# Weight forms split two at a time, and two up tiles of every three taken in seven products (a hybrid retention, gating and conv-MLP layer)

## The chip, the cores and the metric

The kernel runs on one core of a Trainium2 chip. The metric is the device time of one execution in microseconds, taken as the median of three runs. Beside it there is one execution recorded by the hardware profiler; its rows are what the working below is made of.

The engines are named as the profile names them: PE is the matrix engine (TensorE; PEld its weight loads), DVE the vector engine (VectorE), ACT the scalar engine (ScalarE), POOL is GpSimd, and SP the engine that issues most of the transfers. "Instruction on line 85" is written L85.

## What is computed

The layer takes x of 512 tokens by 1024 features in float32 and has two halves:

```python
def reference(x, ...):
    h = _rmsnorm(x, g_pre_mix)
    proj = h @ w_in
    q, k, v, g, u, sv, a_ret, a_sgu = jnp.split(proj, ...)
    y_ret = _retention_branch(q, k, v, g, ret_decay_logit, w_ret_o)
    y_sgu = _sgu_branch(u, sv, sgu_ln_g, sgu_ln_b, w_spatial, b_spatial, w_sgu_o)
    merged = jax.nn.sigmoid(a_ret) * y_ret + jax.nn.sigmoid(a_sgu) * y_sgu
    x = x + _rmsnorm(merged @ w_out, g_post_mix)
    h2 = _rmsnorm(x, g_pre_ffn)
    x = x + _rmsnorm(_conv_gated_mlp(h2, w_up, conv_w, conv_b, w_down), g_post_ffn)
    return x

def _conv_gated_mlp(h, w_up, conv_w, conv_b, w_down):
    hid = h @ w_up                          # 1024 -> 5632
    hid = ... three-tap convolution over the tokens, per feature ... + conv_b
    a, b = jnp.split(hid, 2, axis=-1)
    return (jax.nn.gelu(a) * b) @ w_down    # 2816 -> 1024
```

The change concerns above all the up product `h @ w_up` of the second half.

## The kernel before

**Three matmuls per product.** Every matrix is float32. The matrix engine reads it as two parts in its faster format: `hi`, a copy in that format, and `lo`, what is left (`split`, L83 to L85: the copy on ScalarE at L78, the subtraction on VectorE at L85). A product then takes hi·hi, hi·lo and lo·hi. All weights are loaded as float32 tiles of 128 x 1024 (512 KB) and split on the way.

**The weight stream.** The list `units` (L92 to L116) says in which order weights are used. `w_get` (L198) hands out the next unit and prepares those ahead of it: it goes on until about eight to ten slots' worth of units (`LOOK` = 4) is prepared. A unit of size 2 takes two slots (hi and lo of 1024 columns), a single form of size 1 takes one. Raw weights go through four buffers (`raw_tile`, L119), the split ones through nine slots (`slot`, tag w4, L122). Three kinds of unit matter here. `blk` is one weight tile of 128 output features, whole. `q` and `t` are the two units of a pair in the down product: `q` has the weights as they come (768 columns to split), `t` four sums of them (1024 columns). The third kind are the forms of a pair.

**A pair and a block.** An output tile of 128 features by 512 tokens can be made as a *block* (`f_block`, L635): 8 steps over the 1024 input features, three matmuls of 512 columns each, 24 in all. Two such tiles can be made together as a *pair* (`Pair`, L646 to L705): the product of 1024 x 256 weights with 1024 x 512 activations is cut two by two and made in seven half-size products in place of eight (the Strassen-Winograd scheme), each of four steps with three matmuls of 256 columns: 84 matmuls of 256 columns in place of 48 of 512. The seven weight matrices are the *forms* B11, B21, T1, T2, T3, T4, B22, four of them sums of the others. `w_form` (L152 to L170) makes each when it comes up: B11 loads two raw tiles; T1 computes T1 and T3 on VectorE (L163, L164) and starts T2 on GpSimd (L165); T4 is a GpSimd add as well (L167). Every form is split by itself, 512 columns at a time, into one slot. `part1` makes four products and the first half of the results (the add at L679), `part2` one product (the subtraction at L690), `part3` the last two products (the subtraction at L702). The activations' forms S1 to S4 are made once, by `h2_forms`. The `u` stage and the two gate stages ahead use the same class, four pairs in each, with the gate stages laying two blocks into each pair.

**The up stage.** There are 22 gated tiles (NF), each of two 128-feature output tiles, one of the `a` half and one of the `b` half. Tiles 0 to 3 and 20 and 21 are two blocks each. Tiles 4 to 19 are taken in *couples* (COUPLES, L38): tile i is a pair, tile i + 1 two blocks, and the blocks lie between the pair's parts, so that the forms have time to be made:

```python
            p.part1()
            o = [f_block(h2h, h2l, KD)]
            p.part2()
            o.append(f_block(h2h, h2l, KD, p.part3))   # part3 in the middle of this block
            tile_done(i, p.t)
            tile_done(i + 1, o)
```

`tile_done` (L972) takes a tile through the convolution (`conv`, L928: one scaling on ScalarE, then two steps over 511 columns on VectorE, L933 and L937, for each of its two halves) and the gate (`gated`, L943: the activation on ScalarE, a product on VectorE at L946). At some tiles (7, 11, 13, 17, and from 19 on) it also makes the activation forms of one pair of gated tiles for the down product (`down_forms`, L953: some ten operations on VectorE, L959 to L962 and splits).

**The down product.** 22 tiles are taken as nine pairs (`products`, one `q` and one `t` unit each, seven products of two token tiles with three matmuls each, 42 of 256 columns a pair, L1033) and four whole tiles, twice, for the two halves of the output features.

**What sets the order.** The program is written as one stream; the framework orders each engine's instructions by its own schedule and adds the waits. On each engine instructions run in that order. Buffers are reused round robin: the matrix engine's results lie in eight banks, `tmp` tiles (pair results, convolution results) in six buffers. The transfers of the weights are issued by SP in the stream's order, each as soon as a raw buffer is free.

Of the kernel before, what the change touches and what calls it, by code (L numbers as in the profile page):

```python
# [13 lines left out]
ALU = mybir.AluOpType  # L14

P = 128
# [18 lines left out]
WHOLE = NF - 2 * DP  # L35
EAGER = 7
UP0 = DOWN0 - 2 * NF
COUPLES = [(i, i + 1) for i in range(4, 20, 2)]  # L38

PRE, FFNG, LNG, LNB = 0, 8, 16, 24  # L40
CW, CB = 32, 32 + 3 * 2 * NF
# [5 lines left out]
def tile_block(ctx: ExitStack, tc, xT, x, wall, par, cs, wsp, bsp, gpost, gffn, out):  # L47
# [14 lines left out]
    def tmp(n="tmp", shape=(P, S)):  # L62
        return sb.tile(list(shape), F32, tag="tmp", bufs=6, name=nm(n))
# [19 lines left out]
    def split(hi, lo, src):  # L83
        copy(hi, src)
        nc.vector.tensor_sub(lo, src, as32(hi))  # L85
# [2 lines left out]

    RES1 = NW - 22 - 44
    RES0 = RES1 - RES_OUT  # L90
    FORMS = ("B11", "B21", "T1", "T2", "T3", "T4", "B22")
    units = []  # L92
    i = 0
    while i < NW:
        pair = [(f, i) for f in FORMS]
        if U0 <= i < GATE0:
            units += pair
            i += 2
        elif GATE0 <= i < GATE1:
            units += pair[:4] + [("blk", i + 2)] + pair[4:] + [("blk", i + 3)]  # L100
            i += 4
        elif i == UP0 + 2 * COUPLES[0][0]:
            for a, b in COUPLES:
                pair = [(f, UP0 + 2 * a) for f in FORMS]
                units += pair[:4] + [("blk", UP0 + 2 * b)] + pair[4:] + [("blk", UP0 + 2 * b + 1)]
            i = UP0 + 2 * COUPLES[-1][1] + 2
        elif i == DOWN0:
            for _ in range(2):
                pairs = [[("q", i + j), ("t", i + j)] for j in range(DP)]
                whole = [[("blk", i + DP)], [("blk", i + DP + 1)]]  # L110
                for u in pairs[:4] + whole[:1] + pairs[4:6] + whole[1:] + pairs[6:] if i == DOWN0 else pairs + whole:
                    units += u
                i += DP + WHOLE // 2
        else:
            units.append(("blk", i))
            i += 1  # L116
    w_ready, w_pos, w_held, w_raw = {}, [0, 0], [0], {}

    def raw_tile():  # L119
        return sb.tile([P, 1024], F32, tag="raw", bufs=4, name=nm("raw"))  # L120

    def slot(n, at=0, w=1024):  # L122
        return sb.tile([P, 1088], F32R, tag="w4", bufs=9, name=nm(n))[:, at : at + w]
# [27 lines left out]

    def w_form(form, i):  # L152

        if form == "B11":
            a, b = raw_tile(), raw_tile()
            nc.sync.dma_start(a, wall[i])
            nc.sync.dma_start(b, wall[i + 1])
            w_raw["B11"], w_raw["B12"] = a[:, :S], a[:, S:]
            w_raw["B22"], w_raw["B21"] = b[:, :S], b[:, S:]
        elif form == "T1":  # L160
            t = raw_tile()
            w_raw["T1"], w_raw["T2"], w_raw["T3"], w_raw["T4"] = t[:, :S], t[:, S:], w_raw["B12"], t[:, S:]
            nc.vector.tensor_add(w_raw["T1"], w_raw["B11"], w_raw["B12"])  # L163
            nc.vector.tensor_add(w_raw["T3"], w_raw["B12"], w_raw["B22"])  # L164
            nc.gpsimd.tensor_tensor(out=w_raw["T2"], in0=w_raw["T1"], in1=w_raw["B22"], op=ALU.add)  # L165
        elif form == "T4":
            nc.gpsimd.tensor_tensor(out=w_raw["T4"], in0=w_raw["T2"], in1=w_raw["B21"], op=ALU.add)  # L167
        w = slot("wf", 16)
        split(w[:, :S], w[:, S:], w_raw[form])
        return w[:, :S], w[:, S:]  # L170

    def w_down(form, i):

# [19 lines left out]
        return w_block(u[1]) if u[0] == "blk" else (w_down if u[0] in "qt" else w_form)(*u)  # L193

    def w_size(u):
        return 2 if u[0] in ("blk", "q", "t") else 1

    def w_get(look=LOOK):  # L198

        i = w_pos[0]  # L200
        w_pos[0] += 1
        room = 2 * look + (2 if w_size(units[i]) == 2 else 0)
        n = sum(w_size(u) for u in units[i : w_pos[1]])
        while w_pos[1] < len(units) and (w_pos[1] <= i or n + w_size(units[w_pos[1]]) <= max(room, 9 if look == LOOK else 0)):
            u = units[w_pos[1]]
            w_ready[w_pos[1]] = w_unit(u)
            w_pos[1] += 1
            n += w_size(u)
        return w_ready.pop(i)
# [425 lines left out]
    def f_block(ah, al, n, between=None):  # L635

        wh, wl = w_get()
        o = ps()
        for k in range(n):
            if between and k == n // 2:  # L640
                between()
            c = slice(k * P, (k + 1) * P)
            mm3(o, wh[:, c], wl[:, c], ah[k], al[k], k == 0, k == n - 1)
        return o

    class Pair:  # L646
# [5 lines left out]
            self.h, self.l, self.forms = a or (xh, xl, forms)  # L652
            self.b = [ps() for _ in range(3)]

        def product(self, b, act, first, w=None):
            wh, wl = w or w_get()
            o = self.b[b][:, T0]
            for k in range(4):
                c = slice(k * P, (k + 1) * P)
                h_, l_ = act(k)  # L660
                for n, (w_, a_) in enumerate(((wh, h_), (wh, l_), (wl, h_))):
                    nc.tensor.matmul(  # L662
                        o, w_[:, c], a_, start=first and k == n == 0, stop=k == 3 and n == 2,
                        skip_group_check=True,
                    )
            return o
# [6 lines left out]

        def part1(self):
            c0, c1 = self.t
            o = self.product(0, self.x(0, T0), True)
            copy(c0[:, T0], o)
            o = self.product(1, self.x(4, T0), True)
            v.tensor_add(c0[:, T0], o, c0[:, T0])  # L679
            self.product(2, self.s("S1"), True)  # L680
            o = self.product(0, self.s("S2"), False)
            copy(c1[:, T0], o)
            if self.scale is not None:
                v.tensor_mul(c0[:, T0], c0[:, T0], self.scale[:, T0])

        def part2(self):
            c0, c1 = self.t
            o = self.product(0, self.s("S3"), False)
            copy(c1[:, T1], o)
            v.tensor_sub(c1[:, T1], self.b[2][:, T0], c1[:, T1])  # L690
            self.w = w_get(), w_get()

        def part3(self):
            c0, c1 = self.t
            o = self.product(0, self.x(4, T1), False, self.w[0])
            if self.scale is None:
                copy(c0[:, T1], o)
            else:
                v.tensor_mul(c0[:, T1], o, self.scale[:, T1])
                nc.scalar.activation(out=c0, in_=c0, func=self.func)  # L700
            o = self.product(2, self.s("S4"), False, self.w[1])
            v.tensor_sub(c1[:, T0], o, c1[:, T0])  # L702
            if self.scale is not None:
                v.tensor_mul(c1, c1, self.scale)
                nc.scalar.activation(out=c1, in_=c1, func=self.func)  # L705
# [265 lines left out]

    def tile_done(i, o):  # L972
        gated(*(conv(t, 2 * i + s_) for s_, t in enumerate(o)))
        if i < COUPLES[-1][1]:
            if i in (7, 11, 13, 17):
                down_forms(len(dforms))
        elif len(dforms) < EAGER:
            down_forms(len(dforms))
# [11 lines left out]
            split(h_, l_, s_)  # L990
            h2forms[n] += [(h_[:, t], l_[:, t]) for t in (T0, T1)]

    couples = dict(COUPLES)
    i = 0
    while i < NF:
        if i in couples:
            p = Pair(None, lambda: tmp("c"), (h2h, h2l, h2forms))
            p.part1()
            o = [f_block(h2h, h2l, KD)]
            p.part2()  # L1000
            o.append(f_block(h2h, h2l, KD, p.part3))
            tile_done(i, p.t)
            tile_done(i + 1, o)
            i += 2
        else:
            o = []
            for e in (2 * i, 2 * i + 1):
                o.append(early_o[e] if e < EARLY else f_block(h2h, h2l, KD))
            tile_done(i, o)
            for k in {0: (0,), 1: (2,)}.get(i, ()):  # L1010
                h2_forms(k)
            i += 1
# [150 lines left out]
def _parts(a, n, w):  # L1163

    k = a.shape[0] // P
    return a.reshape(k, P, n, w).transpose(2, 1, 0, 3).reshape(n, P, k * w)
# [11 lines left out]
def _inter(a, b):  # L1178
    return np.stack([a, b], 1).reshape(2 * a.shape[0], *a.shape[1:])


def _two(a):

    b = _parts(a, 8, P).reshape(4, 2, P, 2, S)
    return np.stack([
        np.concatenate([b[:, 0, :, 0], b[:, 1, :, 0]], -1), np.concatenate([b[:, 1, :, 1], b[:, 0, :, 1]], -1),
    ], 1)


def _up(a):  # L1190

    for i, _ in COUPLES:
        b, c = a[2 * i].reshape(P, 2, S), a[2 * i + 1].reshape(P, 2, S)
        a[2 * i : 2 * i + 2] = np.stack([
            np.concatenate([b[:, 0], c[:, 0]], -1), np.concatenate([c[:, 1], b[:, 1]], -1),
        ])
    return a


def _gates(a, w):  # L1200

    return np.concatenate([_two(a), _parts(w, 8, P).reshape(4, 2, P, 1024)], 1).reshape(16, P, 1024)


def _quads(a):
# [76 lines left out]
```

## Time and profile before

| | |
|---|---|
| median of three runs | 830.31 us (830.2 to 830.32) |
| the profiled execution | 831.73 us, its span 830.0 us |
| granted TensorE clock in it | 0.997 |
| start of tile 4 in the up stage | 523.42 us |
| start of the down product | 712.08 us |

The profile is read as follows. A row of a timeline is: start, duration (both us), engine, line, operation, the tile written and the tiles read, shape. On a pipelined engine durations of neighbours overlap, so the cost of an instruction in a dense stretch is the distance to the next start. A row of the chain is start, duration, engine, tile, line and count. A row of the waits is engine, tile and line that waited, on what, and then total, times and longest in us. A row of the windows is the stretch, its length, and for each engine its busy time with the count of instructions, then the granted clock, the DMA engines' share and GB/s.

### The profile page before, as it was taken

How to read it: one execution, taken by the hardware profiler on the slowest of the kernel's cores; microseconds unless marked ns; L12 is line 12 of the kernel's file. 1: busy time of each engine (PE TensorE's matmuls, PEld its weight loads, DVE VectorE, ACT ScalarE, POOL GpSimd, SP SyncE). 2: the span in 40 equal slices, each digit the busy share in tenths (PEclk: the TensorE clock that was granted, in tenths of full speed). 3: DMA queues.
4: the chain of work that ended last, by engine and by line, in shares of the span. 5: the costliest groups of instructions: out<-in, count | busy, mean ns of one | idle time of the engine just before them, and what ended most of it. 6: DMA issues, size and time to landing. Idle time of an engine off the chain costs nothing.

```text
span 830.0 us, 13260 instructions
## 1 busy us (share of the span) xinstructions
PE 819.0 (99%) x5152; PEld 738.5 (89%) x5152; DVE 657.9 (79%) x1100; ACT 439.6 (53%) x769; POOL 101.4 (12%) x102
## 2 busy tenths in 40 slices
PE   9999999999999999999999999999999999999995
PEld 7888888888899999999988898899999998999995
DVE  7479898877898777767765568979799889987967
ACT  6635445546665444444445685556566566554531
POOL 0010000102121111132211211210201200000001
PEclk9999999999999999999999999999999999999998
DMA  8733222213233332233359111233233341233344
GB/s 289 248 115 102 77 77 76 77 51 101 69 101 126 102 102 88 91 101 102 104 162 339 46 54 61 102 102 102 102 102 102 102 153 51 77 115 106 118 147 153
DMA packets 29215, 93.24 MB, mean 112 GB/s; under 512 B 3360, under 2 KB 4000, under 8 KB 29152
## 3 DMA queue, kind: packets, MB, share of 16 engines
q1 hardware_dynamic: 26928, 86.85, 31.5%
q0 software_dynamic: 1360, 4.46, 1.6%
q10 hardware_dynamic: 864, 1.09, 0.4%
q8 instruction: 40, 0.66, 0.3%
q14 instruction: 23, 0.19, 0.1%
HBM read 88.19 MB, written 4.19 MB: 111 GB/s over the span
## 4 chain that ended last, share of the span: by engine, by line
PE 91%; DVE 6%; issue 1%; ACT 1%; POOL 0%; DMA 0%; POOLq 0%; ACTq 0%; DVEq 0%
PE ps L662 24%; PE ps L212 12%; PE ps L213 12%; PE ps L214 12%; PE ps L1033 8%; PE ps L473 5%; PE ps L474 5%; PE ps L475 5%; PE ps L812 2%; PE ps L810 2%; PE ps L811 2%; PE ps L735 1%; DVE fl L85 1%; PE ps L274 1%; DVE dl L85 1%
## 5 line engine op out<-in xcount | busy, mean ns | idle before, releaser
L85 DVE TENSOR_TENSOR wl<-raw,wh 128x1024 fp32r<-128x1024 f32 (+1 forms) x93 | 108.0, 1171 | 52.7 <-PE ps L662 29.4
L78 ACT ACTIVATE wf<-raw 128x512 fp32r<-128x512 f32 x140 | 85.0, 627 | 98.0 <-PE ps L213 41.4
L85 DVE TENSOR_TENSOR wf<-raw,wf 128x512 fp32r<-128x512 f32 x140 | 108.7, 791 | 25.3 <-ACT wf L78 24.1
L662 PE MATMUL ps<-sh,wf 128*128 128x256 f32 x640 | 122.5, 281 | 0.0
L78 ACT ACTIVATE wh<-raw 128x1024 fp32r<-128x1024 f32 (+2 forms) x95 | 93.2, 990 | 38.5 <-DMA raw<-wall 18.5
L662 PEld LDWEIGHTS ps<-sh,wf 128*128 128x128 f32 x640 | 101.7, 188 | 0.8 <-ACT u L78 0.2
L212 PE MATMUL ps<-h2h,wh 128*128 128x512 f32 (+1 forms) x256 | 92.7, 365 | 0.3 <-ACT h2h L880 0.3
L213 PE MATMUL ps<-h2l,wh 128*128 128x512 f32 (+1 forms) x256 | 92.7, 364 | 0.0
L214 PE MATMUL ps<-h2h,wl 128*128 128x512 f32 (+1 forms) x256 | 92.5, 362 | 0.0
L662 PE MATMUL ps<-sl,wf 128*128 128x256 f32 x320 | 89.9, 281 | 0.0
L473 PE MATMUL ps<-wh,xh 128*128 128x512 f32 x192 | 75.0, 391 | 0.0
L474 PE MATMUL ps<-wl,xh 128*128 128x512 f32 x192 | 74.9, 390 | 0.0
L475 PE MATMUL ps<-wh,xl 128*128 128x512 f32 x192 | 74.8, 390 | 0.0
L165 POOL TENSOR_TENSOR raw<-raw,raw 128x512 f32<-128x512 f32 x20 | 36.7, 1834 | 237.1 <-DVE raw L163 182.1
L662 PEld LDWEIGHTS ps<-sl,wf 128*128 128x128 f32 x320 | 61.3, 192 | 0.6
L1033 PE MATMUL ps<-dl,fh 128*128 128x256 f32 x216 | 60.0, 278 | 0.1
L1033 PE MATMUL ps<-dh,fh 128*128 128x256 f32 x216 | 59.9, 277 | 0.0
L1033 PE MATMUL ps<-dh,fl 128*128 128x256 f32 x216 | 59.9, 277 | 0.0
L662 PE MATMUL ps<-xh,wf 128*128 128x256 f32 x288 | 55.3, 282 | 0.0
L214 PEld LDWEIGHTS ps<-h2h,wl 128*128 128x128 f32 x256 | 48.2, 189 | 7.7
L212 PEld LDWEIGHTS ps<-h2h,wh 128*128 128x128 f32 x256 | 48.1, 189 | 7.4 <-ACT h2h L880 0.5
L213 PEld LDWEIGHTS ps<-h2l,wh 128*128 128x128 f32 x256 | 48.3, 189 | 6.6
(306 smaller groups left out, 2046.8 us busy)
## 6 DMA issues: line engine op xcount, KB each, us to landing
raw<-wall SPq DMA_DIRECT2D x145, 512.0 KB, 3.6
x<-x SPq DMA_DIRECT2D x24, 256.0 KB, 5.9
xT<-xT SPq DMA_DIRECT2D x8, 256.0 KB, 5.4
x<-x POOLq DMA_DIRECT2D x8, 256.0 KB, 2.4
xT<-xT POOLq DMA_DIRECT2D x4, 256.0 KB, 3.9
out<-zg SPq DMA_DIRECT2D x4, 256.0 KB, 2.3
out<-zs ACTq DMA_DIRECT2D x3, 256.0 KB, 2.5
cs<-cs SPq DMA_DIRECT2D x2, 256.0 KB, 4.2
```

Source lines behind the costliest of these rows:

```text
L78: nc.scalar.activation(out=o, in_=i, func=AF.Copy)
L85: nc.vector.tensor_sub(lo, src, as32(hi))
L165: nc.gpsimd.tensor_tensor(out=w_raw["T2"], in0=w_raw["T1"], in1=w_raw["B22"], op=ALU.add)
L212: nc.tensor.matmul(o, ah, bh, start=start, stop=False)
L213: nc.tensor.matmul(o, ah, bl, start=False, stop=False)
L214: nc.tensor.matmul(o, al, bh, start=False, stop=stop)
L473: nc.tensor.matmul(acc[t], xh[k][:, c], wh[:, f], start=k == 0, stop=False)
L474: nc.tensor.matmul(acc[t], xh[k][:, c], wl[:, f], start=False, stop=False)
L475: nc.tensor.matmul(acc[t], xl[k][:, c], wh[:, f], start=False, stop=k == KD - 1)
L662: nc.tensor.matmul(o, w_[:, c], a_, start=first and k == n == 0, stop=k == 3 and n == 2, skip_group_check=True,)
L810: nc.tensor.matmul(o, ah, bh, start=k == 0, stop=False)
L1033: nc.tensor.matmul(o, a_[:, c], w_[:, f], start=j == t == i == 0, stop=j == DP - 1 and i == 2 and n not in (M2, M3, M4), skip_group_check= ...
```

## The change

Two things change.

First, the forms of a pair are split two at a time. The unit list has four units for a pair in place of seven: X is B11 with its neighbour as it lies in the raw tile (1024 columns), Y is T1 and T2 side by side (1024), Z is T3 (512), W is T4 and the other raw half (1024). All four sums are made when Y comes up: two on VectorE, two on GpSimd one behind the other. Y's copy and subtraction read T2 and so wait for the first of GpSimd's adds. With that the raw weights no longer need to be laid out by halves on the host (`_two` and `_up` are gone). `product` takes the pair of slots and which half of it to use. This holds for the `u` and gate stages too.

Second, the up stage's tiles 4 to 18 are taken in five *triples* in place of couples: tile i is a pair, tile i + 1 two blocks, tile i + 2 a second pair, whose last part comes after the first part of the next triple (`late`). Tiles 19 and 20 remain a pair and a tile of two blocks (`SINGLE`), and tile 21 is two blocks. The up stage so has eleven pairs (it had eight) and the whole kernel 23 (it had 20). The tiles at which `down_forms` is called stay the same.

```diff
-COUPLES = [(i, i + 1) for i in range(4, 20, 2)]
+TRIPLES = range(4, 19, 3)
+SINGLE = TRIPLES[-1] + 3
...
+    def pair(i):
+        return [(f, i) for f in "XYZW"]
+    def beside(a, i, b=()):
+        return a[:2] + [("blk", i)] + a[2:] + list(b[:2]) + [("blk", i + 1)] + list(b[2:])
...
-            for a, b in COUPLES:
-                pair = [(f, UP0 + 2 * a) for f in FORMS]
-                units += pair[:4] + [("blk", UP0 + 2 * b)] + pair[4:] + [("blk", UP0 + 2 * b + 1)]
+            for a in TRIPLES:
+                e = UP0 + 2 * a
+                units += beside(pair(e), e + 2, pair(e + 4))
+            units += beside(pair(e + 6), e + 8)
...
-        if form == "B11":
-            a, b = raw_tile(), raw_tile()
+        if form == "X":
+            a, b = w_raw["a"], w_raw["b"] = raw_tile(), raw_tile()
             nc.sync.dma_start(a, wall[i])
             nc.sync.dma_start(b, wall[i + 1])
...
-        w = slot("wf", 16)
-        split(w[:, :S], w[:, S:], w_raw[form])
-        return w[:, :S], w[:, S:]
+            raw = a
+        elif form == "Y":
+            a, b, raw = w_raw["a"], w_raw["b"], raw_tile()
+            nc.vector.tensor_add(raw[:, :S], a[:, :S], b[:, :S])
+            nc.vector.tensor_add(a[:, :S], b[:, :S], b[:, S:])
+            nc.gpsimd.tensor_tensor(out=raw[:, S:], in0=raw[:, :S], in1=b[:, S:], op=ALU.add)
+            nc.gpsimd.tensor_tensor(out=b[:, :S], in0=raw[:, S:], in1=a[:, S:], op=ALU.add)
+        elif form == "Z":
+            w = slot("wf", 16)
+            split(w[:, :S], w[:, S:], w_raw["a"][:, :S])
+            return w[:, :S], w[:, S:]
+        else:
+            raw = w_raw["b"]
+        hi, lo = slot("wf", 16), slot("wf", 16)
+        split(hi, lo, raw)
+        return hi, lo
...
     def w_size(u):
-        return 2 if u[0] in ("blk", "q", "t") else 1
+        return 1 if u[0] == "Z" else 2
...
-        if i in couples:
-            p = Pair(None, lambda: tmp("c"), (h2h, h2l, h2forms))
-            p.part1()
+        if i in TRIPLES or i == SINGLE:
+            a, b = up_pair(), None
+            a.part1()
+            if late:
+                late.part3()
+                tile_done(i - 1, late.t)
+                late = None
             o = [f_block(h2h, h2l, KD)]
-            p.part2()
-            o.append(f_block(h2h, h2l, KD, p.part3))
-            tile_done(i, p.t)
+            a.part2()
+            if i != SINGLE:
+                late = up_pair()
+                late.part1()
+                a.part3()
+                tile_done(i, a.t)
+                o.append(f_block(h2h, h2l, KD))
+                late.part2()
+            else:
+                o.append(f_block(h2h, h2l, KD, a.part3))
+                tile_done(i, a.t)
             tile_done(i + 1, o)
-            i += 2
+            i += 3 if late else 2
```

## What I expected, and why

> **What bounds the kernel now.** I read the page first (busy times, the slices, the share of the chain of waits), then TensorE's waits.
>
> ```profile
> PE 819.0 (99%) x5152; PEld 738.5 (89%) x5152; DVE 657.9 (79%) x1100; ACT 439.6 (53%) x769; POOL 101.4 (12%) x102
> ...
> DVE  7479898877898777767765568979799889987967
> ...
> PE 91%; DVE 6%; issue 1%; ACT 1%; POOL 0%; DMA 0%; POOLq 0%; ACTq 0%; DVEq 0%
> ```
> ```profile
> PE ps L259 <- DVE raw L254: 1.0, 1, 1.0
> PE ps L598 <- DVE o L608: 0.3, 1, 0.3
> PE ps L212 <- ACT h2h L880: 0.3, 1, 0.3
> PE ps L274 <- DVE wh L145: 0.2, 1, 0.2
> ```
>
> TensorE (PE) works for 819.0 of 830.0 us, holds 91% of the chain, and its four listed waits add up to 1.8 us. So every product removed is worth its full time, as long as its weights are ready. Who could fail to have them ready is VectorE (DVE), whose average of 79% hides full stretches. The windows show them: the first is one couple (tiles 14 and 15) in the up stage, the next two run across the change from the up to the down product, and the fourth is the rest of the down product.
>
> ```profile
> core 0: us, PE busy (x) PEld busy (x) DVE busy (x) ACT busy (x) POOL busy (x), PEclk, DMA share, GB/s
> 627.69:648.54 20.85, 20.85 (x134) 18.91 (x134) 20.17 (x32) 13.05 (x24) 2.94 (x2) 1.00 0.31 95
> 690.24:711.00 20.76, 20.76 (x94) 17.17 (x93) 20.61 (x37) 11.88 (x19) 0.00 (x0) 1.00 0.16 52
> 711.00:740.00 29.00, 28.91 (x241) 28.55 (x240) 28.86 (x53) 16.52 (x26) 0.59 (x1) 1.00 0.23 72
> 740.00:808.00 68.00, 68.00 (x601) 68.00 (x601) 54.44 (x86) 31.87 (x48) 0.54 (x1) 1.00 0.40 133
> ```
>
> Between 690 and 740 DVE is busy for 49.5 of 49.8 us. It splits the last up weights and the first down weights and forms the seven pairs of activations. It comes through just in time: the last row of that run, and TensorE's first product that needs it, are
>
> ```profile
> 690.06 1.22 DVE L85 TENSOR_TENSOR wl<-raw,wh 128x1024 fp32r<-128x1024 f32 x1
> ...
> 738.51 2.08 DVE L85 TENSOR_TENSOR dl<-raw,dh 128x1024 fp32r<-128x1024 f32 x2
> 739.78 5.28 PE ps L1033 x44
> ```
>
> The first of the two splits in 738.51 ends near 739.65, and TensorE starts at 739.78. In the up stage the lead is thin as well (20.17 of 20.85). TensorE bounds the kernel, with DVE a hair behind it from tile 14 to the fifth pair of the down product.
>
> **The change on TensorE.** A couple, in the chain, is a pair cut by two blocks:
>
> ```profile
> 523.42 5.66 PE ps L662 x48
> ...
> 534.54 1.42 PE ps L662 x12
> ...
> 538.70 2.83 PE ps L662 x24
> ...
> 544.27 5.66 PE ps L662 x48
> ```
>
> The pair is 5.66 + 1.42 + 2.83 = 9.91 us (84 products of 256 columns, 0.118 each). The couple is 544.27 - 523.42 = 20.85, so the two blocks of a tile are 10.94 (48 products of 512 columns, 0.228 each). Each tile moved from blocks to a pair saves 1.03 us. Eight up pairs become eleven (4, 6, 7, 9, 10, 12, 13, 15, 16, 18, 19), 84 - 48 = 36 more products each, 108 in all, and TensorE saves 3 x 1.03 = 3.09 us if it is always fed. A triple takes 2 x 9.91 + 10.94 = 30.76.
>
> The Trainium skill's page "TensorE: Matmul & The Clock Gate", section "Wait — 56ns, not 53.3ns?", has back-to-back warm matmuls start N/2.4 ns plus about 2.5 ns apart, an estimate of 109.2 ns at 256 columns and 215.7 at 512. By that the saving would be 3 x (48 x 215.7 - 84 x 109.2) = 3.5 us. The rows here are 118 and 228 ns, so the rows' 3.09 stands.
>
> **The change on DVE.** What an operation costs in a dense row is its distance to the next start:
>
> ```profile
> 629.45 0.74 DVE L937 SCALAR_TENSOR_TENSOR cv<-c,part,cv 128x511 f32<-128x511 f32 x1
> 630.11 0.74 DVE L937 SCALAR_TENSOR_TENSOR cv<-ps,part,cv 128x511 f32<-128x511 f32 x1
> ...
> 634.89 1.22 DVE L85 TENSOR_TENSOR wl<-raw,wh 128x1024 fp32r<-128x1024 f32 x1
> 636.03 0.41 DVE L960 TENSOR_TENSOR fs<-fs,gp 128x256 f32<-128x256 f32 x1
> 636.36 0.68 DVE L85 TENSOR_TENSOR fl<-gp,fh 128x512 fp32r<-128x512 f32 x1
> 636.97 0.41 DVE L961 TENSOR_TENSOR gp<-gp 128x256 f32<-128x256 f32 x1
> ```
> ```profile
> 714.88 0.94 DVE L85 TENSOR_TENSOR dl<-raw,dh 128x768 fp32r<-128x768 f32 x1
> 715.75 0.68 DVE L946 TENSOR_TENSOR gp<-cv,cv 128x512 f32<-128x512 f32 x1
> ```
>
> That is 0.66 for a conv step, 1.14 for 1024 columns, 0.87 for 768, 0.60 for 512 (636.36 to 636.97) and 0.335 for 256. A pair in seven single splits cost 7 x 0.60 + 2 x 0.60 (the adds) + 3 x 0.335 = 6.4; in forms two at a time it costs 3 x 1.14 + 0.60 + 1.20 + 1.0 = 6.2. So merging saves about 0.2 per pair. But a tile of two blocks cost only 2 x 1.14 = 2.3, so each of the three added pairs brings some 3.9 us to DVE, before its two GpSimd (POOL) adds. Those are not free either:
>
> ```profile
> 640.96 1.65 POOL L165 TENSOR_TENSOR raw<-raw,raw 128x512 f32<-128x512 f32 x1 [16.79 <-DVE raw L163]
> ...
> 641.71 1.45 DVE L85 TENSOR_TENSOR wf<-raw,wf 128x512 fp32r<-128x512 f32 x1
> ```
> ```profile
> 227.55 1.77 POOL L165 TENSOR_TENSOR raw<-raw,raw 128x512 f32<-128x512 f32 x1 [4.14 <-DMA raw<-wall]
> ...
> 228.09 1.78 DVE L85 TENSOR_TENSOR wf<-raw,wf 128x512 fp32r<-128x512 f32 x1
> 229.79 0.41 DVE L679 TENSOR_TENSOR u<-ps,u 128x256 f32<-128x256 f32 x1
> ```
>
> A split that meets such an add is held until the add is over: 1.45 in place of a plain 0.60 is 0.85 lost; 228.09 to 229.79 is 1.70, so 1.1. I take their mean, 1.0, for each add; the largest loss is a whole add of the second kind, L167's 1.29:
>
> ```profile
> 644.07 1.29 POOL L167 TENSOR_TENSOR raw<-raw,raw 128x512 f32<-128x512 f32 x1 [1.47 <-DVE wf L85]
> ```
>
> The Trainium skill's page "SBUF — State Buffer", section "🔬 SBUF: two separate sides", gives the mechanism: VectorE's operations with two SBUF inputs share a port pair with GpSimd under a lock held for the whole instruction, and the second to issue waits. The 1.78 agrees; the rule adds no term.
>
> Now one triple, from the order in which the built program issues DVE's work, between the closing subtractions of two pairs a triple apart (tiles 10 and 13): 8 rows of 1024, 11 of 256, 12 conv steps and 12 of 512. 8 x 1.14 + 11 x 0.335 + 12 x 0.66 + 12 x 0.60 = 27.9. Four POOL adds bring 4.0. One wait for a transfer comes on top: the next pair's second raw weights take the buffer of the block just split, and only four DVE rows (2.4 us) lie between, against a landing time of
>
> ```profile
> raw<-wall SPq DMA_DIRECT2D x145, 512.0 KB, 3.6
> ```
>
> so 1.2 us. Together 33.1 against TensorE's 30.76: DVE loses 2.4 per triple. The first triple begins with forms in hand and loses about 0.8 (an estimate from the same adding up); three more lose 2.4 each, 7.1. The stretch to the last product of tile 19's pair (6 x 1.14 + 14 x 0.335 + 12 x 0.66 + 9 x 0.60 + 0.87 = 25.7, its POOL adds being over by then) meets 27.8 of TensorE and gives 2.1 back. DVE is 0.8 + 7.1 - 2.1 = 5.8 us late there. With 0.85 an add it is 4.0, with 1.1 it is 7.0, with 1.29 it is 9.3; without the transfer's wait and at 0.85, 0.4.
>
> **Where up turns into down.** Without lateness tile 19's pair ends at 523.42 + 5 x 30.76 - 2.83 (the late pair's end is pushed behind the next start) + 20.94 (pair 19 up to its end, that late end, and the one and a half blocks between) = 695.3, and the down product begins at 695.3 + 2.73 + 10.94 = 709.0 (before: 712.1). TensorE comes to the t form of the fourth down pair after 144 products of 0.118, at 726.0. DVE, between that closing subtraction and the end of that t form's split, has 4 x 1.14 + 24 x 0.335 + 11 x 0.66 + 21 x 0.60 + 3 x 0.87 = 35.1 us of rows. It starts some 0.2 after the product, so it ends at 695.5 + 0.3 + 35.1 = 730.9. TensorE waits 4.9 us there even if DVE came on time. The same adding up for the kernel before puts the split that ends near 739.65 at 739.45, which is why I trust it. There the run of full DVE cost nothing; the change brings its end forward by the 3.09 that TensorE saves, and puts more of the fourth pair's work and a late split ahead of it. Lateness from the up stage is simply added. From there on 54.44 of 68 us are used, so TensorE bounds again, and what was lost stays lost: -3.09 + 4.9 + 5.8 = +7.6 us.
>
> The rest I cost at nothing. The transfers are the same in number, SP's queue too. In the u and gate stages the pairs stay twelve; there DVE has room:
>
> ```profile
> 205.00:250.00 45.00, 44.72 (x336) 42.10 (x335) 38.09 (x55) 27.38 (x50) 12.23 (x9) 1.00 0.30 95
> ```
>
> Y's one copy now waits for the POOL add to end (227.55 + 1.77 = 229.32), then some 1.0 for the copy on ScalarE and 1.22 for the split, 231.5, where T1 alone was done at 229.8. Behind that copy on ScalarE stand the conv scalings and the copies out of PSUM, for which DVE's conv steps wait; ScalarE is at 13 of 20.85 in a couple, so it catches up. If the forms held in advance (LOOK) don't cover that 1.7, it is paid once: 0 to +1.7.
>
> The profiled execution took 831.73 us, 830.0 of it span; the median of the runs is 830.31, 1.4 below. The sum is a difference made in the trace, and I put it on the median: 830.3 + 7.6 = 837.9.
>
> **The rivals.**
> - *DVE keeps up* (-3.1, 827.2). For it: DVE's total is only 79%, and before it ran at 20.17 of 20.85 without a single listed wait. Against: 35.1 us of rows in 30.5.
> - *Only the turn costs* (-3.09 + 4.9, 832.1): POOL's adds fall beside DVE's PSUM reads, and the transfers land early. Its up stage would show 27.9 of 30.76.
> - *Full blocking* (1.1 to 1.29 per add): +8.8 to +11.1, 839.1 to 841.4. For it: the changed POOL adds follow one another, so more DVE rows meet them.
> - *The change doesn't do what it says*: 830.3. The built program holds 108 products more, which speaks against it.
>
> **How the numbers follow.** The sum with 0.85 to 1.0 an add holds 0.50, at 837.9 (836.1 to 837.9 and what the 1.7 adds). Only the turn, or little more, 0.20. Full blocking 0.15. Keeping up, 0.10; no change, 0.05. Slower is then 0.85 less what falls within 0.2% (1.7 us, about what a measurement of this kernel can tell from no change): the turn's 832.1 lies just beyond, and I give 0.04 of it to that band. Faster 0.10, same 0.09, slower 0.81. The range goes from 831.0, just under the turn alone, to 843.1, full blocking with the 1.7.
>
> **What would show it.** Products up by 108. In the windows of the up stage, DVE full from about 580 to 745 and the first PE waits from the two-form splits of tile 15's and tile 18's pairs (about 631 and 662); each triple from the second on taking 33 us; then PE waiting for dl and fl between 720 and 740; DVE's share of the chain well above 6%. It is wrong if PE has no waits in the triples, if DVE's splits beside POOL take 0.6, or if the down product begins at 709 and nothing waits behind it.

## The result, and the profile after

| | before | changed |
|---|---|---|
| median | 830.32 us (829.9 to 831.3, six runs) | 845.3 us (843.69 to 848.2, six runs) |
| ratio, with its 95% interval | | 1.0175 [1.0154, 1.0197] |
| profiled execution | 831.73 us, span 830.0 | 843.69 us, span 841.9 |

The change costs 15.0 us by the medians. Slower was forecast, with 837.9 us and a range up to 843.1. The page of the changed kernel, its engines' busy times, the slices of VectorE and the shares of the chain of waits:

```profile
PE 819.6 (97%) x5260; PEld 742.6 (88%) x5260; DVE 676.0 (80%) x1061; ACT 440.5 (52%) x727; POOL 115.7 (14%) x108
...
DVE  7489888867887777777765679799899899987967
...
PE 10%; DVE 3%; issue 0%; POOL 0%; ACT 0%; POOLq 0%; DVEq 0%
```

The 108 products more are there (5260 against 5152). PE is busy for as long as before in a longer span; DVE's slices 27 to 36 are all 8 or 9. The chain could only be followed back to 722.8 us, so its shares can't be set beside those of before, and my sign "DVE's share well above 6%" can't be read from them. TensorE's waits, engine and line, what it waited for, total, times and longest:

```profile
PE ps L674 <- ACT c L79: 4.1, 4, 2.8
PE ps L1061 <- ACT dh L79: 3.7, 3, 2.2
PE ps L674 <- DVE wf L86: 2.0, 1, 2.0
PE ps L271 <- DVE raw L266: 1.0, 1, 1.0
PE ps L1061 <- DVE dl L86: 0.9, 1, 0.9
```

Before, they came to 1.8 us; here the five largest come to 11.7. L674 is the pair's product, L1061 the down product's. Two of the five lines name ScalarE, but ScalarE is not what is short: its copies stand behind others that wait for VectorE. That can be seen at the longest stall. In ScalarE's timeline the copy out of PSUM that TensorE waits for (652.34) stands behind a split's copy that VectorE's subtraction released:

```profile
648.58 0.77 ACT L944 ACTIVATE cv<-ps,part 128x512 f32<-128x512 f32 x1
651.28 0.63 ACT L79 ACTIVATE fh<-fs 128x512 fp32r<-128x512 f32 x1 [1.92 <-DVE fs L974]
651.82 0.61 ACT L958 ACTIVATE cv<-cv 128x512 f32<-128x512 f32 x1
652.34 0.36 ACT L79 ACTIVATE c<-ps 128x256 f32<-128x256 f32 x1
```

The windows answer to those of before. The first three are triples, each from one pair's closing subtraction to that of the pair three tiles later (tile 7's to 10's, to 13's, to 16's); then the stretch to tile 19's, the turn up to the product that needs the fourth down pair's t form, what follows it, and the rest:

```profile
core 0: us, PE busy (x) PEld busy (x) DVE busy (x) ACT busy (x) POOL busy (x), PEclk, DMA share, GB/s
575.56:609.64 34.08, 33.69 (x229) 31.12 (x228) 31.90 (x44) 19.84 (x31) 6.99 (x5) 1.00 0.30 93
609.64:642.95 33.31, 30.61 (x216) 28.36 (x215) 31.89 (x44) 19.61 (x31) 6.99 (x5) 1.00 0.29 95
642.95:677.69 34.74, 31.98 (x216) 29.94 (x215) 31.89 (x44) 20.06 (x31) 6.99 (x5) 0.95 0.29 92
677.69:704.47 26.78, 26.53 (x175) 23.88 (x174) 26.68 (x43) 17.27 (x27) 1.24 (x1) 1.00 0.31 99
704.47:740.27 35.80, 31.05 (x200) 27.96 (x198) 35.73 (x66) 22.14 (x36) 0.00 (x0) 0.95 0.18 60
740.27:750.00 9.73, 9.72 (x71) 9.73 (x72) 9.73 (x18) 4.33 (x7) 0.59 (x1) 0.82 0.36 118
750.00:808.00 58.00, 58.00 (x514) 58.00 (x514) 46.49 (x77) 27.53 (x44) 0.54 (x1) 1.00 0.35 117
```

Read DVE's column against the length. In each triple DVE works 31.9 us and is idle for 2.2, 1.4 and 2.9. At the turn it is full, 35.73 of 35.80, and after 750 it has room again. The granted clock, 1.00 in every such row of before, falls below 1.00 in three.

To compare runs I use one number: DVE's *lateness*, the start of tile 19's closing subtraction minus that of tile 4's first product, minus the 171.9 us that this takes when TensorE never waits (695.33 - 523.42). The 171.9 us are an estimate from the prediction's rows, good to some 0.2 us. The two rows here:

```profile
521.97 0.28 PE L674 MATMUL ps<-h2h,wf 128*128 128x256 f32 x1
```
```profile
704.47 0.42 DVE L716 TENSOR_TENSOR c<-ps,c 128x256 f32<-128x256 f32 x1
```

182.5 - 171.9 = 10.6 us, where the prediction had 5.8.

### The profile page after: what moved, and what is told of

It reads as the page before. It is cut to its first block, busy times and chain, and to the rows that moved or that the text cites. A ratio compares the mean times of both kernels' runs of the same rounds, so it can differ in the third digit from the quotient of the medians.

```text
span 841.9 us, 13454 instructions
## 1 busy us (share of the span) xinstructions
PE 819.6 (97%) x5260; PEld 742.6 (88%) x5260; DVE 676.0 (80%) x1061; ACT 440.5 (52%) x727; POOL 115.7 (14%) x108
## 5 line engine op out<-in xcount | busy, mean ns | idle before, releaser
L674 PE MATMUL ps<-sh,wf 128*128 128x256 f32 x736 | 142.5, 282 | 6.3 <-ACT c L79 3.9
L79 ACT ACTIVATE wf<-raw 128x1024 fp32r<-128x1024 f32 (+1 forms) x92 | 87.3, 950 | 89.3 <-PE ps L225 32.3
L86 DVE TENSOR_TENSOR wf<-raw,wf 128x1024 fp32r<-128x1024 f32 (+1 forms) x92 | 108.3, 1178 | 22.6 <-ACT wf L79 20.6
L674 PEld LDWEIGHTS ps<-sh,wf 128*128 128x128 f32 x736 | 118.0, 189 | 8.4 <-ACT c L79 4.6
L674 PE MATMUL ps<-sl,wf 128*128 128x256 f32 x368 | 103.5, 281 | 0.0
L224 PE MATMUL ps<-h2h,wh 128*128 128x512 f32 (+1 forms) x208 | 73.9, 358 | 0.2 <-ACT h2h L894 0.2
L225 PE MATMUL ps<-h2l,wh 128*128 128x512 f32 (+1 forms) x208 | 73.9, 357 | 0.0
L226 PE MATMUL ps<-h2h,wl 128*128 128x512 f32 (+1 forms) x208 | 73.9, 356 | 0.0
L674 PEld LDWEIGHTS ps<-sl,wf 128*128 128x128 f32 x368 | 70.7, 192 | 0.7
L1061 PE MATMUL ps<-dh,fh 128*128 128x256 f32 x216 | 59.9, 282 | 3.5 <-ACT dh L79 3.3
L1061 PE MATMUL ps<-dl,fh 128*128 128x256 f32 x216 | 60.9, 283 | 0.9 <-DVE dl L86 0.9
L1061 PE MATMUL ps<-dh,fl 128*128 128x256 f32 x216 | 60.6, 282 | 0.0
L674 PE MATMUL ps<-xh,wf 128*128 128x256 f32 x288 | 54.9, 282 | 0.0
L674 PE MATMUL ps<-h2h,wf 128*128 128x256 f32 x264 | 50.3, 281 | 0.3 <-ACT c L79 0.3
L79 ACT ACTIVATE dh<-raw 128x768 fp32r<-128x768 f32 (+1 forms) x36 | 33.7, 948 | 28.0 <-PE ps L1061 12.9
L674 PEld LDWEIGHTS ps<-xh,wf 128*128 128x128 f32 x288 | 45.5, 188 | 0.7 <-ACT g L619 0.2
```

Of the source, the lines that this page charges most:

```text
L79: nc.scalar.activation(out=o, in_=i, func=AF.Copy)
L224: nc.tensor.matmul(o, ah, bh, start=start, stop=False)
L225: nc.tensor.matmul(o, ah, bl, start=False, stop=False)
L226: nc.tensor.matmul(o, al, bh, start=False, stop=stop)
L674: nc.tensor.matmul(o, w_[:, c], a_, start=first and k == i == 0, stop=k == 3 and i == 2, skip_group_check=True,)
L1061: nc.tensor.matmul(o, a_[:, c], w_[:, f], start=j == t == i == 0, stop=j == DP - 1 and i == 2 and n not in (M2, M3, M4), skip_group_check= ...
```

## The experiments

All ratios are to the kernel before on the same chip. The runs were made on three chips, on which the kernel before took 831.64 us (e1 to e4), 832.07 (e5 to e8) and 833.27 (e9 to e11), so medians of different groups are compared by their distance from these.

| run | median, us | ratio, 95% interval | lateness, us |
|---|---|---|---|
| couples, forms two at a time (e1) | 831.48 | 1.0002 [0.9987, 1.0017] | |
| triples, single forms (e2) | 854.49 | 1.0269 [1.0243, 1.0295] | 17.0 |
| no GpSimd adds (e3) | 835.36 | 1.0042 [1.0029, 1.0055] | 1.6 |
| five raw buffers (e4) | 837.8 | 1.0072 [1.0045, 1.0099] | 6.1 |
| turn filled (e5) | 844.92 | 1.0166 [1.0144, 1.0187] | 9.8 |
| adds on VectorE (e6) | 837.61 | 1.0066 [1.0047, 1.0086] | 2.1 |
| five eager forms (e7) | 837.88 | 1.008 [1.006, 1.01] | 10.7 |
| adds, raw buffers, eager forms together (e8) | 829.77 | 0.9973 [0.9962, 0.9983] | 1.4 |
| couples, adds and eager forms (e9) | 833.35 | 1.0009 [0.9995, 1.0023] | |
| e8 with four raw buffers (e10) | 831.6 | 0.9987 [0.9969, 1.0006] | 3.2 |
| the changed kernel again (e11) | 845.16 | 1.0155 [1.0124, 1.0185] | 10.9 |

**Which half of the change costs.** e1 keeps the new forms and goes back to couples:

```diff
-            for a in TRIPLES:
+            for a in COUPLES:                      # range(4, 20, 2)
                 e = UP0 + 2 * a
-                units += beside(pair(e), e + 2, pair(e + 4))
-            units += beside(pair(e + 6), e + 8)
+                units += beside(pair(e), e + 2)
```

> Forms two at a time, but the up stage in couples as before (8 up pairs). My theory, that the three added pairs overfill VectorE and that merging the forms costs nothing: 829 to 831 us, within 1 us of the kernel before, no TensorE wait over 0.5 us in the up stage, VectorE's full run at the turn to the down product ending within 1 us of 739.7. Rival, that Y's wait for GpSimd and the copies queued behind it are what costs: 833 us or more, TensorE waits on ScalarE's copies already in the couples.

No wait over 0.3 us is left in the up stage, and the time is that of before. So splitting two at a time, with Y's wait for GpSimd in it, costs nothing while VectorE has room. e2 does the reverse, triples with the seven single forms of before:

```diff
+                one, two = [(f, e) for f in FORMS], [(f, e + 4) for f in FORMS]
+                units += one[:4] + [("blk", e + 2)] + one[4:] + two[:4] + [("blk", e + 3)] + two[4:]
```

> Five triples as in the changed kernel (11 up pairs), but each form split by itself as before. Theory: the pairs are the cause, so this is slow too: 843 to 849 us, VectorE full from about 580 to 740 and the closing subtraction of tile 19's pair some 10 us late. Rival, that the merged forms are the cause: at most 835 us.

It is slower by more than I expected, 22.9 us, with these waits:

```profile
PE ps L667 <- ACT c L80: 11.6, 7, 4.5
```

So the added pairs, in the order of triples in which they come, are the cause, and the new forms are not. But the merging, which I valued at 0.2 us a pair, is worth 6.4 us of lateness (17.0 against 10.6) over the eleven pairs, some 0.6 each. What makes up that difference was not taken apart.

**GpSimd's adds.** e3 leaves T2 and T4 out:

```diff
-                nc.vector.tensor_add(raw[:, :S], a[:, :S], b[:, :S])
+                nc.vector.tensor_add(raw, a, b)
                 nc.vector.tensor_add(a[:, :S], b[:, :S], b[:, S:])
-                nc.gpsimd.tensor_tensor(out=raw[:, S:], in0=raw[:, :S], in1=b[:, S:], op=ALU.add)
-                nc.gpsimd.tensor_tensor(out=b[:, :S], in0=raw[:, S:], in1=a[:, S:], op=ALU.add)
```

> The changed kernel, but in the up stage T2 and T4 are left out: T1 comes from one add over 1024 columns on VectorE (0.54 us more a pair), T4 is taken as the raw weights, and GpSimd does nothing there. Theory, that GpSimd's four adds a triple hold VectorE for 4.0 us: a triple loses 2.9 us less, VectorE is on time or up to 1 us late at tile 19's last product, the 4.9 us at the turn and one clock drop (1.6) stay: 833 to 836 us. Rival, that the waits for the second raw weights are the cause: these stay, the lateness stays at 6 us or more, 841 us or more.

835.36 us and 1.6 us late: in the range. The rival is out: VectorE still waits 5.0 us for raw weights between 523 and 704 us, where it waited 9.2 in the changed kernel, and yet the lateness is nearly gone. The turn's waits stay, as they should:

```profile
PE ps L1065 <- ACT dh L79: 4.5, 3, 2.1
...
PE ps L1065 <- DVE dl L86: 0.9, 1, 0.9
```

e6 makes T2 and T4 on VectorE:

```diff
+            eng = nc.vector if i >= UP0 else nc.gpsimd
-            nc.gpsimd.tensor_tensor(out=raw[:, S:], in0=raw[:, :S], in1=b[:, S:], op=ALU.add)
-            nc.gpsimd.tensor_tensor(out=b[:, :S], in0=raw[:, S:], in1=a[:, S:], op=ALU.add)
+            eng.tensor_tensor(out=raw[:, S:], in0=raw[:, :S], in1=b[:, S:], op=ALU.add)
+            eng.tensor_tensor(out=b[:, :S], in0=raw[:, S:], in1=a[:, S:], op=ALU.add)
```

> The changed kernel with T2 and T4 of the up stage made on VectorE in place of GpSimd (two adds of 0.60 more a pair). Theory, that a GpSimd add costs VectorE 1.0 us, more than the 0.60 of making it there: a triple is 1.6 us shorter on VectorE, tile 19's last product is about 4 to 5 us late in place of 10.6: 837 to 841 us. Rival, that GpSimd's adds run beside VectorE for the greater part: 846 us or more.

More work on the full engine, and less time: 5.5 us above the kernel before on its chip, in place of 15.0. The lateness falls to 2.1, further than the 4 to 5 expected. VectorE's wait for raw weights falls with it, from 9.2 us to 0.4, so not all of the 8.5 us are the adds' own; why that wait goes was not looked into. The rows of the changed kernel show what an add on GpSimd costs, first GpSimd's two adds, then VectorE's rows beside them:

```profile
627.71 1.58 POOL L172 TENSOR_TENSOR raw<-raw,raw 128x512 f32<-128x512 f32 x1 [16.83 <-DVE raw L170]
630.58 1.66 POOL L173 TENSOR_TENSOR raw<-raw,raw 128x512 f32<-128x512 f32 x1 [1.29 <-DVE raw L171]
```
```profile
628.05 1.79 DVE L947 SCALAR_TENSOR_TENSOR cv<-c,part,cv 128x511 f32<-128x511 f32 x1
...
630.37 0.74 DVE L951 SCALAR_TENSOR_TENSOR cv<-c,part,cv 128x511 f32<-128x511 f32 x1
631.03 2.29 DVE L86 TENSOR_TENSOR wf<-raw,wf 128x1024 fp32r<-128x1024 f32 x1
```

A conv step takes 1.79 in place of 0.74 and a split of 1024 columns 2.29 in place of 1.22: 1.05 and 1.07 lost. Over a triple, DVE's 31.9 us of busy time are the 27.9 of its rows, as the prediction adds them up, and 4.0 more for four adds, the prediction's term to the tenth.

**The second raw weights.** e4 gives the raw weights a fifth buffer and takes two other buffers away for the room:

```diff
-NBLK = 76
+NBLK = 74
-        return sb.tile([P, 1024], F32, tag="raw", bufs=4, name=nm("raw"))
+        return sb.tile([P, 1024], F32, tag="raw", bufs=5, name=nm("raw"))
```

> The changed kernel with five raw weight buffers in place of four. Theory, that the wait for the pair's second raw weights (7.2 us in four places) is a part of the lateness beside GpSimd's 4.0 a triple: that wait goes, VectorE is about 6 us less late at tile 19, 837 to 841 us. Rival, that this wait only takes up time in which VectorE would wait for something else: 843 us or more.

837.8 us, and lateness down by 4.5 to 6.1. VectorE's waits between 523 and 704 us, first the changed kernel's, then e4's:

```profile
DVE raw L170 <- DMA raw<-wall: 9.2, 5, 2.8
```
```profile
DVE raw L170 <- DMA raw<-wall: 4.2, 4, 1.6
DVE wf L86 <- ACT wf L79: 3.8, 3, 2.3
```

The wait is halved rather than gone, but what goes is part of the lateness. This wait is where most of the lateness was mis-sized: 2.2, 1.4 and 2.9 us in the three triples, not 1.2 in each, which is 2.9 of the 4.8 us that were missing. The rows of the longest, the issues of the pair's two transfers by SP and then the add that waits for the second:

```profile
666.69 0.33 SPq L165 DMA_DIRECT2D raw<-wall  x1
668.39 0.33 SPq L166 DMA_DIRECT2D raw<-wall  x1
```
```profile
673.58 0.69 DVE L170 TENSOR_TENSOR raw<-raw,raw 128x512 f32<-128x512 f32 x1 [2.82 <-DMA raw<-wall]
```

The second is issued 1.7 us after the first, and 5.2 us pass until its data is used. Landing took 5.1 of them; in the other two triples, with the same 1.7 us between the issues, it took 4.4 and 3.6. The second loads that were issued 4.3 us or more after the first landed after 3.3 to 3.5. I had taken 3.6, the median over all 145 transfers, which hides this.

**The turn.** e7 makes two of the seven eager pairs of activation forms later:

```diff
-EAGER = 7
+EAGER = 5
```

> The changed kernel with five pairs of activation forms made ahead of the down product in place of seven; the other two are made later, in the down product. Theory, that the 35.1 us of VectorE's work at the turn set the wait there: 7.0 us of it go, TensorE reaches the t form of the fourth pair with a wait some 7 us shorter, and VectorE has the room later: 836 to 840 us. Rival, that what is moved is missed later: 843 us or more.

837.88 us, in the expected range. The lateness stays (10.7), and TensorE's only wait at the turn is 0.5 us for a whole tile's weights. So the 35.1 us of VectorE's work there is a bound of its own, beside the lateness.

**The clock.** TensorE's rows around the longest stall, and around the resumption at 740.27:

```profile
649.72 0.28 PE L674 MATMUL ps<-sh,wf 128*128 128x256 f32 x1
652.75 0.58 PE L674 MATMUL ps<-sh,wf 128*128 128x256 f32 x1 [2.76 <-ACT c L79]
653.13 0.41 PE L674 MATMUL ps<-sl,wf 128*128 128x256 f32 x1
653.35 0.63 PE L674 MATMUL ps<-sh,wf 128*128 128x256 f32 x2
```
```profile
738.67 0.73 PE L1061 MATMUL ps<-dh,fh 128*128 128x256 f32 x4 [1.03 <-ACT dh L79]
740.27 0.39 PE L1061 MATMUL ps<-dl,fh 128*128 128x256 f32 x1 [0.87 <-DVE dl L86]
740.50 0.28 PE L1061 MATMUL ps<-dh,fl 128*128 128x256 f32 x1
...
742.38 0.41 PE L1061 MATMUL ps<-dl,fh 128*128 128x256 f32 x1
742.59 0.41 PE L1061 MATMUL ps<-dh,fl 128*128 128x256 f32 x1
...
744.72 0.28 PE L1077 MATMUL ps<-wl,fh 128*128 128x256 f32 x1
744.84 0.28 PE L1077 MATMUL ps<-wh,fl 128*128 128x256 f32 x1
```

After the longest stall products follow some 0.21 us apart in place of 0.11, and so they do again from 741.3 to 744.7 (742.38 to 742.59), for 3.4 us. Then they are fast again (744.72 to 744.84): for that time the granted clock was halved. The Trainium skill's page "TensorE: Matmul & The Clock Gate", section "Part 1: The HAM clock gate", has this: the clock falls to half after an idle window of some 3.4 us and returns after a busy one as long, and windows run freely. The halving and its length agree; but here 2.76 us of waiting was enough, and ahead of 741 two waits of 1.0 and 0.9. Nor does every wait of that size do it: the one of 1.98 us that ended at 633.38 was followed by no fall here, while in e5, e7 and e11 a fall comes within 2 us after the same wait. I had no term for it. e5 puts products whose result isn't used where TensorE waited:

```diff
+            if n == 3 and j in fill:                       # fill = (2, 3)
+                ah, al = dforms[j]["A11"]
+                for r in range(18):
+                    nc.tensor.matmul(m[M8][:, T0], ah[:, :P], (wh, wl)[r % 2][:, :256], start=True, stop=True, ...)
```

> The changed kernel with 36 products more: 18 ahead of the t form of the third and 18 ahead of that of the fourth down pair, written to a bank that isn't in use yet, so that TensorE works (2.1 us each) where it waited. Theory, that the granted clock falls to half after the two stalls there (730 and 740) and that the second fall costs 1.6 us beyond VectorE's lateness: no clock under 1.00 between 700 and 760, the t form of the fourth pair still at about 740 us, 842 to 844.5 us in spite of 4.2 us more work. Rival, that the clock plays no part: 845 to 849.5 us.

The stretch of 9.73 us after the wait for the t form, to be read against the changed kernel's row 740.27:750.00 above:

```profile
740.90:750.63 9.73, 9.73 (x85) 9.73 (x86) 9.73 (x18) 4.34 (x7) 0.59 (x1) 1.00 0.35 120
```

85 products at a clock of 1.00, against 71 at 0.82: 14 products, 14 x 0.113 = 1.6 us. So much the clock cost in the stretch after the turn. From tile 4's first product to the last one it is 309.1 us with 36 products more, and 310.6 without (832.54 - 523.40 and 832.56 - 521.97). By the median (844.92) the two can't be told apart, and it lies just above the range that I gave to this theory, so the time alone does not settle it; the rows do, for this place. Some 0.9 us of the 1.6 was given back between the two halves of the down product, where e5's TensorE has two waits (at 781.7 and 782.9) that the changed kernel's has not; so by e5 the total would be only some 0.7 us shorter without that fall. The first two falls of the clock lie where VectorE sets the pace, and what they cost wasn't measured. e11 repeats the changed kernel:

> The changed kernel once more, unchanged, on the chip of the two others. Theory: VectorE's lateness at tile 19 comes out the same within 1 us (10.6 from the start of tile 4), while the clock falls after other stalls than in the first profile: 843 to 848 us.

845.16 us, and 10.9 us late. Two falls of the clock come at other places, 620 to 640 and 640 to 660 us in place of 640 to 660 and 720 to 740; the third is after the turn again:

```profile
620.00:640.00 20.00, 18.02 (x119) 16.86 (x118) 18.32 (x27) 10.26 (x16) 3.24 (x2) 0.91 0.28 94
640.00:660.00 20.00, 18.14 (x119) 16.98 (x119) 19.54 (x29) 12.84 (x21) 3.73 (x2) 0.91 0.22 75
720.00:740.00 20.00, 14.96 (x122) 14.12 (x122) 19.93 (x39) 10.02 (x18) 0.00 (x0) 1.00 0.16 53
740.00:760.00 20.00, 19.13 (x150) 18.93 (x150) 16.40 (x27) 9.91 (x14) 0.59 (x1) 0.91 0.37 124
```

**A version that gains.** e8 is the changed kernel with the edits of e6, e4 and e7 together.

> T2 and T4 on VectorE, five raw buffers, and five eager forms together. By the sum: a triple is 27.9 + 2.4 = 30.3 us on VectorE against TensorE's 30.76, the turn 28.4 against 30.5, so TensorE is fed and the 3.1 us of saved products show: 827 to 829 us. Rival, that the added pairs stall TensorE elsewhere: 830.5 us or more.

0.9973 [0.9962, 0.9983], 829.77 us where the kernel before took 832.07 on that chip. Across the turn TensorE is full, beside a VectorE that is full too:

```profile
704.00:740.00 36.00, 36.00 (x284) 34.77 (x283) 36.00 (x63) 22.64 (x34) 0.00 (x0) 1.00 0.25 87
```

From tile 4's first product to the last one it takes 293.6 us (818.49 - 524.90), before 297.3 (820.60 - 523.26): the 3.1 us of saved products, 0.3 of the old wait at the turn, and some 0.4, an estimate, because the faster of two paces (last section) begins at 728 us in place of 740. The profiled executions differ by 2.0 us (829.75 against 831.73), the medians by 2.3. Ahead of tile 4 some is lost, since the fifth buffer leaves two others fewer and TensorE waits 1.3 us at the product with w_out (two waits of 0.9 and 0.4). The control e9 has the same edits with couples and four raw buffers:

> Control for the version that combines the parts: eight up pairs in couples as before, with forms two at a time, T2 and T4 on VectorE and five eager forms, four raw buffers. Theory, that only the three added pairs can bring a gain and the other parts only make room for them: within 1 us of the kernel before. Rival, that the rearranged VectorE work is itself the gain: 2 us or more faster than before.

No change by the medians (1.0009). They can't settle it alone, because e9 has the slower pace of the last section throughout, as all of its runs at 833.0 to 833.9 suggest, and the runs of the kernel before on that chip are mixed. But e1 has it too, and from tile 4's first product to the last one e1 takes 300.5 us and e9 300.1: without the pairs the other two edits are worth 0.3 us. So the gain is the pairs' and the other edits only make room. e10 drops the fifth buffer:

> Triples with T2 and T4 on VectorE and five eager forms, but four raw buffers. Theory: VectorE is about 2 us late at tile 19's last product as with the adds alone, the turn's 28.4 us against 30.5 take that up, and the 0.9 to 1.3 us that the fifth buffer (with two other buffers fewer) cost at the product with w_out are gone: 2 to 3.5 us faster than before. Rival, that the fifth buffer is needed: TensorE waits again at the turn, slower than before.

That expectation failed: 0.9987 with an interval that takes in no change. The wait at w_out is gone, but with VectorE 3.2 us late TensorE waits again in the up stage and after the turn:

```profile
PE ps L675 <- DVE wf L86: 1.0, 1, 1.0
PE ps L1078 <- ACT wh L79: 0.7, 1, 0.7
```

## Why the prediction was right and where it failed

- *Saved products.* 108 more of the short ones are there, and e8 shows the 3.1 us when TensorE is fed. Right.
- *VectorE is filled by the added pairs.* e1, e2 and e9 show it: without the pairs, no cost; with them and without merging, more cost. Right.
- *GpSimd's adds, 4.0 us a triple.* Measured 31.9 - 27.9 = 4.0, and e3 and e6 remove most of the lateness with them, though some of the wait for raw weights goes too. The 9.0 us that e3 takes off and the 4.5 of e4 are together more than the 10.6 that there are, so the two causes can't be added up from these runs. Right in size.
- *The wait for the second raw weights, 1.2 us a triple.* This step failed in size, and it is the main one: the median landing time of all loads was taken for that of a load issued 1.7 us behind another. Measured 2.2, 1.4 and 2.9. With it three triples lost 34.08 + 33.31 + 34.74 - 3 x 30.76 = 9.85 us in place of 7.1. The first one lost 1.8 in place of 0.8 (575.56 - 521.97 - 51.8, the last being the time without waits). The last stretch gave back 27.8 - 26.8 = 1.0 in place of 2.1, at least in part because a GpSimd add that I took to be over by then lay in it: the conv step beside it, shown below, took 1.46 us in place of 0.74. 1.79 + 9.85 - 1.02 = 10.6 in place of 5.8.
- *The turn, 4.9 us.* From the closing subtraction to the end of the t form's split I had 0.3 + 35.1 = 35.4; the split ends near 740.14, 35.7 after 704.47. TensorE resumes 218.3 us after tile 4's first product; without waits it would be 202.6. These 15.7 us are the lateness of 10.6 and 5.1 for the turn, and e7 confirms that this work is the bound. Right.
- *The clock, at nothing.* This is the second step that failed: no rival and no term had the clock, and it cost 1.6 us after the turn. The Trainium skill's page "TensorE: Matmul & The Clock Gate" has the rule (section "Part 1: The HAM clock gate"), and stalls of several us were in my own sum.
- *The signs.* The first waits of more than 0.5 us end at 617 and 633 us and the longest at 653, where I had named 631 and 662: VectorE fell behind sooner. The other signs came largely as forecast, except DVE's share of the chain, which can't be read.

```profile
678.02 1.46 DVE L951 SCALAR_TENSOR_TENSOR cv<-c,part,cv 128x511 f32<-128x511 f32 x1
```

By the measured terms: -3.09 + 10.6 + 4.9 + 1.6 = 14.0, less the 0.3 us that the kernel before waits at its own turn, 13.7. The two traces give 310.6 - 297.3 = 13.3 us from tile 4's first product to the last. The profiled execution differs by 12.0 because tile 4 began 1.3 us earlier in it; the six runs lie 0 to 4.5 us above it, so its 843.69 was the fastest of them. What made the others longer isn't known; that some had the slower pace of the last section, as e11's profiled run of 847.81 us had, is possible and not shown. The rivals "DVE keeps up", "only the turn costs" and "no change" are out. "Full blocking" came nearest in time for a wrong reason, since the four adds cost 4.0 us and not more.

## What to carry to other kernels

When an edit takes time off the bounding engine and puts work on the next one, add up the second engine's rows in the order in which they are issued, stretch by stretch, and not its average: VectorE's 79% hid a stretch of 50 us at over 99%, and both that bound (35.4 against 35.7 us) and the cost of blocked operations (4.0 a triple) could be read from the old trace. Take a transfer's landing time from issues that come as close together as the new ones will, and allow for a halved clock after new stalls of TensorE: here stalls of 2 to 2.8 us, and two of some 1 us close together, were followed by 3.4 us of it, though not each time. An add moved off a full engine to GpSimd can cost that engine more than making it itself (1.0 against 0.6 us here).

## What the runs showed of the hardware that was not expected

The down product has two paces at the same granted clock. The kernel before and the control e9 over the same 20 us, where TensorE never waits and the clock is 1.00 in both:

```profile
762.00:782.00 20.00, 20.00 (x179) 20.00 (x178) 19.74 (x34) 11.80 (x27) 0.54 (x1) 1.00 0.36 120
```
```profile
762.00:782.00 20.00, 20.00 (x172) 20.00 (x171) 19.93 (x36) 11.64 (x26) 1.13 (x2) 1.00 0.40 134
```

There are 179 products against 172, and from start to start they are 0.113 us apart against 0.118, which makes some 3 us over the 80 us from 740 on. Every profile begins the down product at 0.118, the distance of the up stage. e1, e7, e9 and e10 keep it; the others change to 0.113, the kernel before with the short pause of TensorE that ends at 739.78, e8 at 728 us. A change back occurs too, in e2 at 792 us and in e11 at 745, and e6 changes three times (at 715, 743 and 775). The kernel before, ahead of its change, has the count of the slower pace:

```profile
715.00:735.00 20.00, 20.00 (x172) 20.00 (x171) 20.00 (x38) 10.68 (x18) 0.00 (x0) 1.00 0.25 79
```

The profile of e10, 833.23 us, has 172 in 762 to 782 too, and its ten runs fall into five near 830.0 and five near 833.2; the runs of the kernel before on that chip reach from 830.28 to 834.82. What sets the pace was not found. The ends of profiles are compared above only where both have the same one from 740 us on, and e10's verdict is as wide as it is probably because of this.
